# Reading the first 2048 rows of a row-sum as one contiguous block, and storing the sums in two pieces

## Chip, cores, metric

One core of one Trainium2 chip runs the kernel. The metric is the device time in microseconds (us) of one execution, lower is better. The granted clock was 1.0.

## The reference

```python
def setup_inputs():
    batch, seq, dim = 32, 512, 1024
    return {"x": np.random.randn(batch, seq, dim).astype(np.float32)}

def reference(x):
    return np.sum(np.maximum(x, 0), axis=-1).astype(np.float32)
```

There are 16384 rows of 1024 floats, 4 KB each: 64 MiB to read and 64 KB to write. Each row gives one sum of its positive elements.

## The kernel before

Each of the 128 partitions owns 128 consecutive rows. Its rows therefore begin 512 KB after those of the partition before it; I call this distance the *pitch*. A load of 16 rows for all partitions moves 8 MiB: from each partition's region it takes one contiguous run of 64 KB. Seven such loads go round three buffers; then come loads of 8, 4, 2 and 1 rows, and two halves of the last row.

```python
xv = x.rearrange("b s d -> (b s) d").rearrange("(p j) d -> p j d", p=P)
ov = out.rearrange("b s -> (b s)").rearrange("(p j) -> p j", p=P)
# ... buffers, semaphores (cut)
for c in range(NBIG + 1):                       # NBIG = 7, NB = 3, BIG = 16
    if c >= NB:
        sp.wait_ge(s_dve, 3 * (c - NB + 1))     # buffer free?
    if c < NBIG:
        sp.dma_start(
            out=buf[:, c % NB, :, :], in_=xv[:, c * BIG : (c + 1) * BIG, :]
        ).then_inc(s_in[c], 16)
# ... small loads of the tail, all issued at once; compute on ACT and DVE (cut)
sp.wait_ge(s_tdve, 1)
sp.dma_start(out=ov[:, :], in_=res[:, :]).then_inc(s_out, 16)
sp.wait_ge(s_out, 16)
```

Of the kernel before, what the change touches and what calls it, by code (L numbers as in the profile page):

```python
# [2 lines left out]

P = 128
D = 1024
BIG = 16
NBIG = 7
NTWO = 6
NB = 3
STEPS = [4, 5, 7]  # L10
MIXED = [3, 4, 5]
TAIL = [8, 4, 2, 1]
LAST = [512, 512]


def bass_relu_sum_kernel(
    nc: bass.Bass,
    x: bass.AP,
    out: bass.AP,
):  # L20





    fp32 = mybir.dt.float32
    ALU = mybir.AluOpType
    AF = mybir.ActivationFunctionType
    X = mybir.AxisListType.X

    B, S, _ = x.shape
    J = B * S // P
    assert BIG * NBIG + sum(TAIL) + 1 == J and sum(LAST) == D

    xv = x.rearrange("b s d -> (b s) d").rearrange("(p j) d -> p j d", p=P)
    ov = out.rearrange("b s -> (b s)").rearrange("(p j) -> p j", p=P)

    buf = nc.alloc_sbuf_tensor("buf", [P, NB, BIG, D], fp32)
    last = nc.alloc_sbuf_tensor("last", [P, LAST[1] + 1], fp32)
    res = nc.alloc_sbuf_tensor("res", [P, J], fp32)  # L40

    n_in = NBIG + len(TAIL) + 2
    s_in = [nc.alloc_semaphore(f"s_in{i}") for i in range(n_in)]
    s_act = nc.alloc_semaphore("s_act")
    s_dve = nc.alloc_semaphore("s_dve")
    s_tact = nc.alloc_semaphore("s_tact")
    s_tdve = nc.alloc_semaphore("s_tdve")
    s_out = nc.alloc_semaphore("s_out")

    sp, act, dve = nc.sync, nc.scalar, nc.vector  # L50


    tb = NBIG % NB
    for c in range(NBIG + 1):
        if c >= NB:
            sp.wait_ge(s_dve, 3 * (c - NB + 1))
        if c < NBIG:
            sp.dma_start(  # L58
                out=buf[:, c % NB, :, :], in_=xv[:, c * BIG : (c + 1) * BIG, :]
            ).then_inc(s_in[c], 16)  # L60
    r = 0
    tail = []
    for i, n in enumerate(TAIL):
        sp.dma_start(  # L64
            out=buf[:, tb, r : r + n, :],
            in_=xv[:, NBIG * BIG + r : NBIG * BIG + r + n, :],
        ).then_inc(s_in[NBIG + i], 16)
        tail.append((r, n, s_in[NBIG + i]))
        r += n
    sp.dma_start(  # L70
        out=buf[:, tb, r, 0 : LAST[0]], in_=xv[:, J - 1, 0 : LAST[0]]
    ).then_inc(s_in[-2], 16)
    sp.dma_start(out=last[:, 0 : LAST[1]], in_=xv[:, J - 1, LAST[0] : D]).then_inc(
        s_in[-1], 16
    )


    def on_act(t, acc):
        return act.activation(t, t, AF.Relu, accum_out=acc)  # L79

    def on_dve(t, acc):
        return dve.tensor_scalar(  # L82
            out=t, in0=t, scalar1=0.0, scalar2=None, op0=ALU.max, op1=ALU.add, accum_out=acc
        )

    def row(c, i):
        return buf[:, c % NB, i, :], res[:, c * BIG + i : c * BIG + i + 1]

    for c in range(NTWO):
        b, steps = c % NB, STEPS if c < NTWO - 1 else MIXED  # L90
        act.wait_ge(s_in[c], 16)
        if steps is MIXED:
            dve.wait_ge(s_in[c], 16)
            for i in (BIG - 4, BIG - 3):
                on_dve(*row(c, i))
        r = 0
        for i, n in enumerate(steps):
            t = buf[:, b, r : r + n, :]
            act.activation(t, t, AF.Relu).then_inc(s_act, 1)  # L99
            dve.wait_ge(s_act, 3 * c + i + 1)  # L100
            dve.tensor_reduce(  # L101
                out=res[:, c * BIG + r : c * BIG + r + n], in_=t, axis=X, op=ALU.add
            ).then_inc(s_dve, 1)
            r += n
        if steps is MIXED:
            for i in (BIG - 2, BIG - 1):
                on_act(*row(c, i))


    j0 = NBIG * BIG  # L110
    for c in range(NTWO, NBIG):
        act.wait_ge(s_in[c], 16)
        dve.wait_ge(s_in[c], 16)
        for i in range(BIG):
            (on_act if i % 2 else on_dve)(*row(c, i))
    for r, n, s in tail:
        if n > 1:
            act.wait_ge(s, 16)
        dve.wait_ge(s, 16)
        for i in range(r, r + n):  # L120
            f = on_act if (i - r) % 2 else on_dve
            f(buf[:, tb, i, :], res[:, j0 + i : j0 + i + 1])

    act.wait_ge(s_in[-2], 16)
    on_act(buf[:, tb, BIG - 1, 0 : LAST[0]], last[:, LAST[1] : LAST[1] + 1]).then_inc(s_tact, 1)
    dve.wait_ge(s_tact, 1)
    dve.wait_ge(s_in[-1], 16)
    on_dve(last[:, :], res[:, J - 1 : J]).then_inc(s_tdve, 1)


    sp.wait_ge(s_tdve, 1)
    sp.dma_start(out=ov[:, :], in_=res[:, :]).then_inc(s_out, 16)
    sp.wait_ge(s_out, 16)


# [1 line left out]
_INS = ['x']  # L137
_OUTS = [((32, 512), 'float32')]


# [21 lines left out]
```

## Time and profile before

| | before |
|---|---|
| median, first three runs | 162.84 us (162.80 to 163.05) |
| profiled span | 161.4 us |
| share of the chain that ended last | DMA 69%, ACT 18%, DVE 10% |
| one 64 KB packet once under way (the trace's DMA records) | 2.418 us |

The page of the kernel before: the DMA share by slices (in tenths, 40 slices), what was moved, and the parts of the chain that ended last.

```profile
DMA  7969979979979979979979979979979979899992
...
HBM read 67.11 MB, written 0.07 MB: 416 GB/s over the span
...
DMA 69%; ACT 18%; DVE 10%; SPq 1%; issue 0%
...
out_dram<-res SPq DMA_DIRECT2D x1, 64.0 KB, 1.5
```

The DMA engines are at it from the first slice to the last but one. The ACT and DVE shares of the chain are no proof of a compute limit: while these pieces ran, the next transfers were already queued. The last line says that the 64 KB store needs 1.5 us from issue to landing; it comes after everything else.

The table of stretches of the kernel before: start and end in us, length, then busy time of DVE, ACT and POOL, clock, DMA share and GB/s. This is the steady part.

```profile
23.10:42.40 19.30, 15.04 (x3) 14.04 (x3) 0.00 (x0) 1.00 1.00 435
42.40:61.90 19.50, 17.66 (x4) 14.07 (x4) 0.00 (x0) 1.00 1.00 430
61.90:81.20 19.30, 17.32 (x4) 14.02 (x3) 0.00 (x0) 1.00 1.00 435
```

DMA share 1.00 at 430 to 435 GB/s while ACT and DVE have time to spare: the loads bound the kernel. The Trainium skill ("DMA: Bandwidth & Descriptors", "Specifications") gives a fabric ceiling of 435 GB/s; sixteen engines at 64 KB in 2.418 us are 434 GB/s, so this trace agrees.

The timeline of the kernel before (start, length, engine, instruction, idle time before it and what ended it): ACT begins the first three transfers as soon as each has landed; the last line is its start on the seventh, which it takes row by row.

```profile
23.13 14.04 ACT L99 ACTIVATE buf<-buf 128x4096 f32<-128x4096 f32 x3 [21.13 <-DMA buf<-in_x_dram]
...
42.44 14.04 ACT L99 ACTIVATE buf<-buf 128x4096 f32<-128x4096 f32 x3 [5.26 <-DMA buf<-in_x_dram]
...
61.88 14.04 ACT L99 ACTIVATE buf<-buf 128x4096 f32<-128x4096 f32 x3 [5.40 <-DMA buf<-in_x_dram]
...
139.27 1.06 ACT L79 ACTIVATE buf<-buf 128x1024 f32<-128x1024 f32 x1 [6.64 <-DMA buf<-in_x_dram]
```

*First data* is ACT's first start, 23.13 us. *Later loads* is the time from there to the start on the seventh transfer at 139.27, 116.14 us: six steps, from the first transfer's landing to the seventh's.

The stretches around the start of the kernel before:

```profile
1.60:2.30 0.70, 0.00 (x0) 0.41 (x1) 0.00 (x0) 1.00 2.79 936
2.30:3.10 0.80, 0.00 (x0) 0.00 (x0) 0.00 (x0) 1.00 1.31 492
```

A packet is booked whole in the stretch where it begins; this is why the share exceeds 1. So the last column counts starts: 492 GB/s x 0.80 us is 6 packets of 64 KB. Six of the 16 DMA engines began their first packet only after 2.3 us; the other ten had begun between 1.73 and 2.3. I call these six *late starts*.

### The profile page before, as it was taken

The numbers are of one execution on the slowest core, as the hardware profiler recorded it, in microseconds if no ns is written. First come the engines' busy times: TensorE is split into PE (matmuls) and PEld (weight loads), VectorE is DVE, ScalarE is ACT, GpSimd is POOL, SyncE is SP. The second block draws the span as 40 slices with busy tenths as digits, with TensorE's granted clock in tenths as the row PEclk, the third lists the DMA queues.
The fourth block names the chain that finished last, engine by engine and source line by source line (L and its number), as shares of the span: only waits on it lengthen the run. The fifth ranks groups of instructions, "written<-read, shape, count | busy, mean of one in ns | idle before, by whom it ended". The sixth has DMA issues, their size and how long they took to land.

```text
span 161.4 us, 143 instructions
## 1 busy us (share of the span) xinstructions
DVE 122.0 (76%) x56; ACT 101.0 (63%) x55; POOL 0.2 (0%) x4
## 2 busy tenths in 40 slices
DVE  0000003998969898798979989699899999598995
ACT  3000029992499906998089960999429980496972
POOL 0000000000000000000000000000000000000000
DMA  7969979979979979979979979979979979899992
GB/s 260 504 292 504 471 341 487 487 325 487 487 325 487 471 309 520 471 309 520 487 309 504 487 325 487 487 325 487 487 325 487 487 325 487 374 422 414 406 406 74
DMA packets 2016, 67.18 MB, mean 416 GB/s; under 512 B 224, under 2 KB 352, under 8 KB 736
## 3 DMA queue, kind: packets, MB, share of 16 engines
q1 hardware_dynamic: 2016, 67.18, 97.0%
HBM read 67.11 MB, written 0.07 MB: 416 GB/s over the span
## 4 chain that ended last, share of the span: by engine, by line
DMA 69%; ACT 18%; DVE 10%; SPq 1%; issue 0%
DMA buf<-in_x_dram 69%; ACT buf L99 17%; DVE res L101 9%; SPq L64 1%; ACT buf L79 0%; DVE last L82 0%; SPq L58 0%
## 5 line engine op out<-in xcount | busy, mean ns | idle before, releaser
L101 DVE TENSOR_REDUCE res<-buf 128x4 f32<-128x4096 f32 (+3 forms) x18 | 100.4, 5603 | 34.9 <-ACT buf L99 34.9
L99 ACT ACTIVATE buf<-buf 128x4096 f32<-128x4096 f32 (+3 forms) x18 | 80.8, 4553 | 47.7 <-DMA buf<-in_x_dram 47.7
L79 ACT ACTIVATE buf<-buf 128x1024 f32<-128x1024 f32 (+1 forms) x18 | 18.4, 1021 | 9.7 <-DMA buf<-in_x_dram 9.7
L82 DVE TENSOR_SCALAR_CACHE_REDUCE buf<-buf 128x1024 f32<-128x1024 f32 x18 | 21.0, 1217 | 2.7 <-DMA buf<-in_x_dram 2.5
L79 ACT ACTIVATION_READ_ACCUMULATOR buf<-buf 128x1 f32 x18 | 3.4, 187 | 0.0
L99 ACT ACT_TABLE_LOAD x1 | 1.3, 1283 | 0.7 <-PEq L147 0.7
L82 DVE DVE_READ_ACCUMULATOR buf<-buf 128x1 f32 x18 | 1.5, 84 | 0.0
L82 DVE TENSOR_SCALAR_CACHE_REDUCE last<-last 128x513 f32<-128x513 f32 x1 | 0.7, 690 | 0.2 <-ACT buf L79 0.2
L147 POOL MEMSET const-bfloat16-1.0<- 128x1 bf16 x1 | 0.1, 102 | 0.0
L147 POOL MEMSET const-uint8-127<- 128x1 uint8 x1 | 0.1, 101 | 0.0
L147 POOL MEMSET const-float32-0.0<- 128x1 f32 x1 | 0.1, 99 | 0.2 <-issue 0.2
L147 POOL MEMSET const-float32-1.0<- 128x1 f32 x1 | 0.1, 98 | 0.0
L82 DVE DVE_READ_ACCUMULATOR last<-last 128x1 f32 x1 | 0.1, 83 | 0.0
## 6 DMA issues: line engine op xcount, KB each, us to landing
buf<-in_x_dram SPq DMA_DIRECT2D x1, 4096.0 KB, 26.7
buf<-in_x_dram SPq DMA_DIRECT2D x1, 2048.0 KB, 31.2
buf<-in_x_dram SPq DMA_DIRECT2D x1, 1024.0 KB, 33.2
buf<-in_x_dram SPq DMA_DIRECT2D x1, 512.0 KB, 34.0
buf<-in_x_dram SPq DMA_DIRECT2D x1, 256.0 KB, 34.1
last<-in_x_dram SPq DMA_DIRECT2D x1, 256.0 KB, 34.3
buf<-in_x_dram SPq DMA_DIRECT2D x7, 36.4
out_dram<-res SPq DMA_DIRECT2D x1, 64.0 KB, 1.5
```

Of the source, the lines that this page charges most:

```text
L64: sp.dma_start(out=buf[:, tb, r : r + n, :], in_=xv[:, NBIG * BIG + r : NBIG * BIG + r + n, :],).then_inc(s_in[NBIG + i], 16)
L79: return act.activation(t, t, AF.Relu, accum_out=acc)
L82: return dve.tensor_scalar(out=t, in0=t, scalar1=0.0, scalar2=None, op0=ALU.max, op1=ALU.add, accum_out=acc)
L99: act.activation(t, t, AF.Relu).then_inc(s_act, 1)
L101: dve.tensor_reduce(out=res[:, c * BIG + r : c * BIG + r + n], in_=t, axis=X, op=ALU.add).then_inc(s_dve, 1)
L147: nc = _bacc.Bacc("TRN2", target_bir_lowering=False, num_devices=1)
```

## The change

The first transfer reads rows 0 to 2047 as one block: 16 rows for each partition, pitch 64 KB. The other 14336 rows are dealt out 112 to a partition, pitch 448 KB. The sums then belong to two regions of the output, hence two stores: the first block's sums (64 B of each partition) are stored early, behind the queued loads, and the others (448 B of each partition instead of 512 B) at the end. The intent can only be at the ends of the load stream, since amount, packet size and compute stay.

```diff
-    xv = x.rearrange("b s d -> (b s) d").rearrange("(p j) d -> p j d", p=P)
-    ov = out.rearrange("b s -> (b s)").rearrange("(p j) -> p j", p=P)
+    xr = x.rearrange("b s d -> (b s) d")
+    of = out.rearrange("b s -> (b s)")
+    x0 = xr[0 : P * BIG, :].rearrange("(p j) d -> p j d", p=P)
+    o0 = of[0 : P * BIG].rearrange("(p j) -> p j", p=P)
+    xv = xr[P * BIG :, :].rearrange("(p j) d -> p j d", p=P)
+    ov = of[P * BIG :].rearrange("(p j) -> p j", p=P)
 ... (semaphore s_out0: cut)
-                out=buf[:, c % NB, :, :], in_=xv[:, c * BIG : (c + 1) * BIG, :]
+                out=buf[:, c % NB, :, :],
+                in_=xv[:, (c - 1) * BIG : c * BIG, :] if c else x0[:, :, :],
 ... (the tail's row numbers less BIG: cut)
+    sp.dma_start(out=o0[:, :], in_=res[:, 0:BIG]).then_inc(s_out0, 16)
 ...
-    sp.dma_start(out=ov[:, :], in_=res[:, :]).then_inc(s_out, 16)
+    sp.dma_start(out=ov[:, :], in_=res[:, BIG:J]).then_inc(s_out, 16)
+    sp.wait_ge(s_out0, 16)
     sp.wait_ge(s_out, 16)
```

More of the change, by code (lines that the diff above doesn't have):

```diff
@@ L47, in bass_relu_sum_kernel @@
     s_tdve = nc.alloc_semaphore("s_tdve")
+    s_out0 = nc.alloc_semaphore("s_out0")
     s_out = nc.alloc_semaphore("s_out")
@@ L65, in bass_relu_sum_kernel @@
             out=buf[:, tb, r : r + n, :],
-            in_=xv[:, NBIG * BIG + r : NBIG * BIG + r + n, :],
+            in_=xv[:, (NBIG - 1) * BIG + r : (NBIG - 1) * BIG + r + n, :],
         ).then_inc(s_in[NBIG + i], 16)
@@ L70, in bass_relu_sum_kernel @@
     sp.dma_start(
-        out=buf[:, tb, r, 0 : LAST[0]], in_=xv[:, J - 1, 0 : LAST[0]]
+        out=buf[:, tb, r, 0 : LAST[0]], in_=xv[:, J - BIG - 1, 0 : LAST[0]]
     ).then_inc(s_in[-2], 16)
-    sp.dma_start(out=last[:, 0 : LAST[1]], in_=xv[:, J - 1, LAST[0] : D]).then_inc(
+    sp.dma_start(out=last[:, 0 : LAST[1]], in_=xv[:, J - BIG - 1, LAST[0] : D]).then_inc(
         s_in[-1], 16
     )
+    sp.dma_start(out=o0[:, :], in_=res[:, 0:BIG]).then_inc(s_out0, 16)
     def on_act(t, acc):
```

## The prediction

> **What bounds the kernel now.** The loads do. In the chain that ended last, DMA has 69% of the span, and its ACT (18%) and DVE (10%) pieces run while later loads are already queued (waits view: ACT waited 47.7 us for loads). The table of stretches shows 430 to 435 GB/s and a DMA share of 1.00 from 23.1 to 120 us. Work on successive 8 MB transfers starts at 23.13, 42.44, 61.88, ..., 139.27 (timeline): 19.3 to 19.4 us each. In the trace's DMA records one 64 KB packet takes 2.418 us almost without exception after the first transfer; 16 engines at that pace are 433 GB/s. Only the two ends can give: the start (first load issued 0.73, usable 23.13, so 22.4 us against 19.35 for later ones: 3.05 us more) and the end (last load usable 158.31, span 161.4: 3.1 us).
>
> **The start in detail (DMA records).** The 16 engines' first packets begin between 1.73 and 2.97 us. The first packet on each took 2.49 to 3.27 us instead of 2.42, and six engines had a slow fifth packet (2.63 to 2.82). The excess over eight regular packets is 0.08 to 1.08 us by engine; the engine that finishes the first transfer last lost 0.76. With no excess and the same starts the transfer would end 34.12 − 33.64 = about 0.5 us earlier (estimate from those records). The engines are busy to the end, so a gain here is kept.
>
> **What the change does.** Bytes, packet size, load count and compute stay. The first transfer's row groups lie 64 KB apart instead of 512 KB; the later ones 448 KB apart. The Trainium skill, "DMA: Bandwidth & Descriptors", section "Latency and other measured facts", reports slow copies at power-of-two row pitches; its inference is channel aliasing of streams in lock step. This trace shows full rate at the 512 KB pitch except in the first packets, when the engines have just started together: estimate −0.1 to −0.5 us, or nothing if that is a cold start which any address pays. The steady part cannot gain.
>
> **The stores.** One more issue on SP (0.4 us) falls in its 34.7 us wait: free. The early store queues behind the last loads and should be done before 160.5. The last store stays on the path: issued 159.79, landed 1.5 us later, 128 runs of 512 B at 27 ns each. It becomes 128 runs of 448 B. The same page, "Specifications", says that below 512 B the DMA engine does a read-modify-write; nothing in this trace shows its cost. Estimate: +0 to +0.5 us (eight runs per engine, up to treble their 27 ns, plus a read).
>
> **Sum.** −0.1 to −0.5 and +0 to +0.5: 162.84 becomes about 162.6 us, 80% range 161.7 to 163.4. Chances: faster by over 2% 0.02, within 2% 0.96, slower by over 2% 0.02.
>
> **What would show each step.** Right: later transfers still 19.3 to 19.4 us apart; the first usable data at 22.6 to 23.0 instead of 23.13; last load to last store issue unchanged (1.5 us); final store 1.5 to 2.0 us to landing. Wrong: first data at 23.1 or later (cold start, not addresses); slow packets reappearing in the second transfer, which is then the first to touch the spread rows; a store above 2 us.
>
> **What would make it wrong.** The engines' late starts may themselves depend on the addresses (gain up to 1 us); neighbouring streams may collide and lengthen the first transfer by microseconds; the early store's short writes may still be in the way of the last one.

## The result, and the profile after

| | before | after | ratio, 95% interval |
|---|---|---|---|
| first comparison | 162.94 us (4 runs) | 162.38 us (4 runs) | 0.9964 [0.9947, 0.9982] |
| repeated later, run r2_after_again | 162.84 us (9 runs) | 162.38 us (5 runs) | 0.9973 [0.9960, 0.9987] |

A ratio is the mean time of one kernel's runs over that of the other's runs of the same rounds, so it is not quite the ratio of the medians quoted. The change is worth 0.44 to 0.59 us (0.27% and 0.36% of about 163 us): clear of the noise. The answering lines of the page after:

```profile
DMA  7979979979979979979979979979979969999992
...
HBM read 67.11 MB, written 0.07 MB: 417 GB/s over the span
...
DMA 69%; ACT 18%; DVE 10%; SPq 1%; issue 0%
...
out_dram<-res SPq DMA_DIRECT2D x1, 56.0 KB, 1.6
```

At this scale nothing has changed. The last store needs 1.6 us where the old one needed 1.5, but before rounding these are 1.56 and 1.54 (issue in the timeline to the last landing record), so the store is hardly longer. The timeline after, same rows as before:

```profile
22.77 14.04 ACT L107 ACTIVATE buf<-buf 128x4096 f32<-128x4096 f32 x3 [20.77 <-DMA buf<-in_x_dram]
...
42.12 14.05 ACT L107 ACTIVATE buf<-buf 128x4096 f32<-128x4096 f32 x3 [5.31 <-DMA buf<-in_x_dram]
...
61.47 14.04 ACT L107 ACTIVATE buf<-buf 128x4096 f32<-128x4096 f32 x3 [5.30 <-DMA buf<-in_x_dram]
...
138.89 1.06 ACT L87 ACTIVATE buf<-buf 128x1024 f32<-128x1024 f32 x1 [6.65 <-DMA buf<-in_x_dram]
```

First data comes at 22.77 instead of 23.13, 0.36 us earlier. The step from the second transfer to the third is 61.47 - 42.12 = 19.35 us instead of 61.88 - 42.44 = 19.44. The sum of later loads is 116.12 instead of 116.14. The stretches around the start, after:

```profile
1.60:2.30 0.70, 0.00 (x0) 0.41 (x1) 0.00 (x0) 1.00 4.40 1498
2.30:3.10 0.80, 0.00 (x0) 0.00 (x0) 0.00 (x0) 1.00 0.00 0
```

All 16 engines begin before 2.3 us; there is no late start. The spans, 161.4 and 161.0 us, differ by about what was won at the first data (0.36 us); the end costs the same: from the landing of the last load on the slowest engine to the end of the span the traces have 161.37 - 158.92 = 2.45 us before and 161.04 - 158.57 = 2.47 after.

But this is one trace of each. What has made the start earlier, and whether that is all, had to be tried.

### The profile page after: what moved, and what is told of

The parts are those of the page before. It is cut to its first block, busy times and chain, and to the rows that moved or that the text cites. A ratio compares the mean times of both kernels' runs of the same rounds, so it can differ in the third digit from the quotient of the medians.

```text
span 161.0 us, 144 instructions
## 1 busy us (share of the span) xinstructions
DVE 122.0 (76%) x56; ACT 101.0 (63%) x55; POOL 0.2 (0%) x4
## 4 chain that ended last, share of the span: by engine, by line
DMA 69%; ACT 18%; DVE 10%; SPq 1%; issue 0%
DMA buf<-in_x_dram 69%; ACT buf L107 17%; DVE res L109 9%; SPq L71 1%; ACT buf L87 0%; DVE last L90 0%; SPq L64 0%
```

## The experiments

Twelve kernels ran, in three calls; those of one call ran on one chip (e1 to e4; e7 to e10; r1, r2, e6 and e11). A ratio is always to the kernel before. For all but two runs (e9 and e10) I give it here and, from the trace, late starts (counted as above), first data and later loads:

| run | pitch of first / later transfers | ratio [95%] | late starts | first data, us | later loads, us |
|---|---|---|---|---|---|
| kernel before, first trace | 512 / 512 KB | 1 | 6 | 23.13 | 116.14 |
| r1_before_again | 512 / 512 | 1.0006 [0.9992, 1.0019] | 5 | 22.97 | 116.08 |
| e1_stores_only | 512 / 512 | 1.0011 [0.9998, 1.0024] | 6 | 22.96 | 116.58 |
| e8_later_448k | 512 / 448 | 0.9990 [0.9974, 1.0006] | 6 | 22.85 | 116.09 |
| changed kernel, first trace | 64 / 448 | 0.9964 [0.9947, 0.9982] | 0 | 22.77 | 116.12 |
| r2_after_again | 64 / 448 | 0.9973 [0.9960, 0.9987] | 2 | 22.68 | 116.08 |
| e2_block_only | 64 / 512 | 0.9971 [0.9958, 0.9985] | 2 | 22.66 | 116.43 |
| e3_block_second | 448, then 64 / 448 | 0.9969 [0.9956, 0.9981] | 0 | 22.73 | 116.12 |
| e7_pitch_508k | 508 / 512 | 0.9980 [0.9965, 0.9995] | 0 | 22.84 | 116.10 |
| e6_pitch_256k | 256 / 512 | 0.9991 [0.9978, 1.0004] | 2 | 22.82 | 116.08 |
| e4_one_block | 0 / 512 | 0.9971 [0.9954, 0.9988] | 0 | 22.01 | 116.42 |
| e11_first_row_alone | 64 / 448 | 0.9998 [0.9986, 1.0011] | not comparable | 22.90 | 116.10 |

My theory after the result was COMPACT: the first transfer now lies in 8 MB instead of being spread over 64 MB, and the engines get going together. The rivals were PITCH (512 KB between row groups is a bad distance, others are better), LATER (the gain is in the later transfers) and STORES.

**e1_stores_only**: loads as before, sums stored in two pieces.

```diff
+    sp.dma_start(out=ov[:, 0:BIG], in_=res[:, 0:BIG]).then_inc(s_out0, 16)
 ... (semaphore s_out0: cut)
-    sp.dma_start(out=ov[:, :], in_=res[:, :]).then_inc(s_out, 16)
+    sp.dma_start(out=ov[:, BIG:J], in_=res[:, BIG:J]).then_inc(s_out, 16)
+    sp.wait_ge(s_out0, 16)
```

> Loads as before, the two stores of the change (correct result). Theories of the 0.36% gain: COMPACT (the first transfer's small address range makes the engines start closer together), PITCH (512 KB between row groups collides, any other pitch is better), LATER (the gain is in the later transfers at 448 KB), STORES (the shorter last store). COMPACT, PITCH and LATER expect 162.8 to 163.1 here, ratio 1.000 within 0.001, first data at 23.1 us. STORES expects 162.4, ratio 0.9965.

Measured: 163.17 us, ratio 1.0011; six late starts and first data at 22.96. STORES falls: the gain is not there. Nor do the stores cost anything visible on the path: from the last load's landing to the end this trace has 161.65 - 159.21 = 2.44 us, against 2.45 before. The first-data expectation of 23.1 was missed by 0.14 us, which says how far single traces differ. Something unexpected: the second transfer took 19.71 us (the lines of the first three transfers in the timeline):

```profile
22.96 14.04 ACT L101 ACTIVATE buf<-buf 128x4096 f32<-128x4096 f32 x3 [20.95 <-DMA buf<-in_x_dram]
...
42.67 14.04 ACT L101 ACTIVATE buf<-buf 128x4096 f32<-128x4096 f32 x3 [5.67 <-DMA buf<-in_x_dram]
...
62.14 14.04 ACT L101 ACTIVATE buf<-buf 128x4096 f32<-128x4096 f32 x3 [5.43 <-DMA buf<-in_x_dram]
```

The DMA records show 18 packets over 2.5 us in this second transfer and 15 in the third. So the part that looked steady is not always steady. That loss is the trace of one execution.

**e2_block_only**: only the first transfer is the block; one store (wrong in 16 sums of each partition).

```diff
+    x0 = x.rearrange("b s d -> (b s) d")[0 : P * BIG, :].rearrange("(p j) d -> p j d", p=P)
-                out=buf[:, c % NB, :, :], in_=xv[:, c * BIG : (c + 1) * BIG, :]
+                out=buf[:, c % NB, :, :],
+                in_=xv[:, c * BIG : (c + 1) * BIG, :] if c else x0[:, :, :],
```

> Only the first transfer reads the contiguous 8 MB; the later ones stay at 512 KB pitch, one store (wrong on purpose in the first 16 sums of each partition). COMPACT and PITCH expect the whole gain: 162.4, ratio 0.9965, first data at 22.7 to 22.8 us, engines' first packets beginning within 0.6 us of each other instead of 1.2. LATER and STORES expect 162.9, ratio 1.000, first data at 23.1.

Measured: 162.50 us, ratio 0.9971, first data at 22.66, two late starts (the last at 2.75 us, so not within 0.6 us as expected):

```profile
2.30:3.10 0.80, 0.00 (x0) 0.00 (x0) 0.00 (x0) 1.00 0.41 164
...
22.66 14.04 ACT L101 ACTIVATE buf<-buf 128x4096 f32<-128x4096 f32 x3 [20.65 <-DMA buf<-in_x_dram]
```

The first transfer's addresses alone carry most of the gain, so LATER cannot be its whole source. In this trace the later loads took 116.43 us, 0.3 us longer than in the changed kernel: something is lost again at 512 KB, though the ratio, 0.9971, does not show it.

**e3_block_second**: the changed kernel with its first two loads exchanged, so that a transfer spread over 56 MB at 448 KB comes first (correct result).

```diff
-                in_=xv[:, (c - 1) * BIG : c * BIG, :] if c else x0[:, :, :],
+                in_=x0[:, :, :] if c == 1 else xv[:, max(c - 1, 0) * BIG : max(c, 1) * BIG, :],
+        k = (1 - c if c < 2 else c) * BIG
-                out=res[:, c * BIG + r : c * BIG + r + n], in_=t, axis=X, op=ALU.add
+                out=res[:, k + r : k + r + n], in_=t, axis=X, op=ALU.add
```

> The changed kernel with its first two loads in the other order: the first one is spread over 56 MB at 448 KB pitch, the contiguous block comes second (correct result). COMPACT expects the gain gone: 162.9, ratio 1.000, first data at 23.1. PITCH expects it kept: 162.4, ratio 0.9965, first data at 22.75. LATER expects it kept too.

Measured: 162.44 us, ratio 0.9969, no late start, first data at 22.73:

```profile
1.60:2.30 0.70, 0.00 (x0) 0.40 (x1) 0.00 (x0) 1.00 4.42 1498
2.30:3.10 0.80, 0.00 (x0) 0.00 (x0) 0.00 (x0) 1.00 0.00 0
...
22.73 14.04 ACT L108 ACTIVATE buf<-buf 128x4096 f32<-128x4096 f32 x3 [20.72 <-DMA buf<-in_x_dram]
```

COMPACT, my own theory, falls: contiguity is not needed. At a pitch of 448 KB a first transfer spread over 56 MB keeps the gain. Whether any pitch other than 512 KB would do is what e7 and e6 ask.

**e4_one_block**: the first transfer reads the same 64 KB for each partition (wrong).

```diff
+    x0 = x.rearrange("b s d -> (b s) d")[0:BIG, :].partition_broadcast(P)
 ... (load line as in e2_block_only)
```

> The first transfer reads the same 64 KB for each of the 128 partitions, the most compact source there is; the rest as before (wrong on purpose in the first 16 sums). COMPACT expects at least the gain of the change, 162.0 to 162.4, ratio 0.994 to 0.9965, and first packets near 2.42 us if their slowness has to do with touching new memory; if the slow first packet (2.8 to 3.3 us) is a start-up cost whatever the address, it stays at that. PITCH in its form 'streams in step meet in the same part of the memory' expects it slower than before: first data at 23.5 us or later, ratio above 1.002.

Measured: 162.31 us, ratio 0.9971. In the DMA records the first packets took 2.52 to 2.59 us, against 2.49 to 3.27 before and 2.82 to 3.63 after. First data came at 22.01, 0.65 us ahead of any kernel that reads distinct rows:

```profile
22.01 14.04 ACT L101 ACTIVATE buf<-buf 128x4096 f32<-128x4096 f32 x3 [20.00 <-DMA buf<-in_x_dram]
...
41.53 14.04 ACT L101 ACTIVATE buf<-buf 128x4096 f32<-128x4096 f32 x3 [5.48 <-DMA buf<-in_x_dram]
```

So the slow first packet is not a fixed cost of starting an engine: it depends on what the sixteen engines read. The expected loss from "streams in step meet in the same part of the memory" did not come; reading literally the same rows is fast. Part of the gain is given back: the second transfer took 19.52 us, against 19.31 to 19.35 in the four traces of the kernels before and after, and later loads 116.42.

**e7_pitch_508k** and **e6_pitch_256k**: the kernel before with the first transfer at another pitch (wrong); the load line is that of e2_block_only.

```diff
+    x0 = x.rearrange("b s d -> (b s) d")[0 : P * 127, :].rearrange("(p j) d -> p j d", p=P)[:, 0:BIG, :]   # e7
+    x0 = x.rearrange("b s d -> (b s) d")[0 : P * 64, :].rearrange("(p j) d -> p j d", p=P)[:, 0:BIG, :]    # e6
```

> The kernel before, with only the first transfer read at a pitch of 508 KB (127 rows) instead of 512 KB, as widely spread as before (wrong on purpose in the first 16 sums). After the run with the block in second place, COMPACT has fallen. PITCH expects the engines' first packets to begin within 0.5 us of each other (1.2 us before), first data at 22.6 to 22.8, and about 162.4 to 162.5 us, ratio 0.996 to 0.9975. A rival, that only the pitches 448 KB and 64 KB happen to suit, would leave starts and first data as before: 23.1, ratio 1.000.

> The kernel before with only the first transfer at 256 KB pitch (wrong on purpose). If it is the power of two that makes the engines meet, late starts stay (last one at 2.5 to 3.0), first data at 22.9 to 23.1, ratio 0.999 to 1.000. If only the full 512 KB is bad, it is as with 508 KB: starts to 2.1, ratio 0.997 to 0.998.

At 508 KB: 162.64 us, ratio 0.9980, clear of noise but just short of the 0.996 to 0.9975 that PITCH expected; no late start, as it expected:

```profile
1.60:2.30 0.70, 0.00 (x0) 0.41 (x1) 0.00 (x0) 1.00 4.58 1498
2.30:3.10 0.80, 0.00 (x0) 0.00 (x0) 0.00 (x0) 1.00 0.00 0
...
22.84 14.04 ACT L101 ACTIVATE buf<-buf 128x4096 f32<-128x4096 f32 x3 [20.83 <-DMA buf<-in_x_dram]
```

But first data came at 22.84, just short of the expected 22.6 to 22.8, and no earlier than with 512 KB on the same chip (22.85 in e8_later_448k). The DMA records show why: the first packets took 2.89 to 3.74 us, on average 3.20 (in e8_later_448k 3.00). Most of what was won at the start was paid in the first packet. The trace of the kernel before shows the other side of this: the ten engines that began early took 3.13 us on average for their first packet, the six late ones 2.80. So late starts alone do not explain the gain. At 256 KB the ratio of 0.9991 (its interval holds 1) and the last start at 2.66 us lie where the power-of-two expectation had them, and first data at 22.82 is 0.08 us earlier than it said; but there are two late starts and not five or six. It is not shown that powers of two are to blame: 64 KB is one too, and e2_block_only keeps the gain with it.

**e8_later_448k**: the changed kernel with the first transfer back at 512 KB (wrong).

```diff
-    x0 = xr[0 : P * BIG, :].rearrange("(p j) d -> p j d", p=P)
+    x0 = xr.rearrange("(p j) d -> p j d", p=P)[:, 0:BIG, :]
```

> The changed kernel with the first transfer put back to 512 KB pitch; the later transfers stay at 448 KB, two stores (wrong on purpose). PITCH of the first transfer expects first data back at 23.0 to 23.1 and most of the gain gone: 162.7 to 163.0, ratio 0.9985 to 1.000. LATER (packets over 2.5 us in transfers 2 to 4 at 512 KB, which neither kernel with 448 KB shows) expects 19.35 us from the second transfer on without exception, and 0.1 to 0.3 us of gain kept: ratio 0.998 to 0.9995. If the whole gain stays, 0.9965, the first transfer's pitch was not the cause.

Measured: 162.73 us, ratio 0.9990 [0.9974, 1.0006]. The six late starts are back:

```profile
1.60:2.30 0.70, 0.00 (x0) 0.40 (x1) 0.00 (x0) 1.00 2.70 936
2.30:3.10 0.80, 0.00 (x0) 0.00 (x0) 0.00 (x0) 1.00 1.38 492
...
22.85 14.04 ACT L107 ACTIVATE buf<-buf 128x4096 f32<-128x4096 f32 x3 [20.85 <-DMA buf<-in_x_dram]
```

Most of the gain is gone with them, going by the ratio itself; its interval is wide. First data at 22.85 is earlier than the expected 23.0 to 23.1. What is kept, some 0.16 us by the ratio, is not clear of noise, and 0.9990 lies in the range of LATER as well as in that of PITCH. From the second transfer on, each took 19.32 to 19.36 us.

**e9_touch_same** and **e10_touch_other**: the kernel before with a small load ahead, waited for, that reads 512 B for each partition: of the row groups that the first transfer will read, or of the first 128 rows of the input (one look each; about 2 us dearer on purpose).

```diff
+    sp.dma_start(out=last[:, 0:128], in_=xv[:, 0, 0:128]).then_inc(s_touch, 16)                               # e9
+    sp.dma_start(out=last[:, 0:128], in_=x.rearrange("b s d -> (b s) d")[0:P, 0:128]).then_inc(s_touch, 16)   # e10
+    sp.wait_ge(s_touch, 16)
 ... (semaphore s_touch: cut)
```

> The kernel before with a small load of the first 512 B of each of the 128 row groups, waited for, ahead of the first transfer (about 2 us dearer on purpose). One look at the packets. If the slow first packet (2.5 to 3.3 us) comes from the first touch of each address region, the first packets of the big transfer are now regular (2.42 to 2.5) and the late starts are gone. If it comes from 16 engines starting together on addresses that collide, it stays at 2.8 to 3.3 and starts still spread over 1.2 us.

> The same, but the small load reads the first 128 rows, one 512 KB stretch, so 127 of the 128 row groups stay untouched. First touch of addresses: first packets slow (2.8 to 3.3) here and regular in the run that touched the same groups. A cost of the queue's or engines' own first use: regular in both. Collision at a common start: slow in both.

Measured: 165.32 and 164.81 us. In the DMA records the first packets of the big transfer took 2.87 to 3.39 us in the one and 2.51 to 3.21 in the other; their starts were spread over 0.95 and 1.20 us. Both stay slow. So neither a first use of the engines nor a first touch of the row groups, as far as 512 B of each touches them, is the cause in these traces (one of each). Of the three expectations that leaves sixteen engines starting together on a set of addresses, which no run isolates. The small load itself gave a second sight of the pitch. Issue to landing, first with a pitch of 512 KB (e9_touch_same):

```profile
last<-in_x_dram SPq DMA_DIRECT2D x1, 64.0 KB, 2.5
```

and with 4 KB (e10_touch_other):

```profile
last<-in_x_dram SPq DMA_DIRECT2D x1, 64.0 KB, 2.0
```

The same 64 KB landed 0.5 us later with the 128 reads of 512 B lying 512 KB apart (one trace of each).

**r1_before_again** and **r2_after_again**: both kernels unchanged, for second traces and for the noise.

> The kernel before, unchanged, for a second trace and for the noise of the comparison: 162.9 to 163.1, ratio 1.000 within 0.001. TWO PARTS (the first transfer at 512 KB costs some 0.25 us by late starts, and the second to fourth transfers at 512 KB some 0.2 us by packets over 2.5 us) expects again engines' first packets up to 2.7 us or later, and from the first transfer's data to the last row of the seventh more than 116.12 us. CHANCE (one trace of each is too few) would show starts within 0.6 us here too.

> The changed kernel, unchanged: 162.4, ratio 0.9955 to 0.9975. TWO PARTS expects starts within 0.6 us, first data at 22.6 to 22.8, no packet over 2.5 us in transfers 2 to 6. CHANCE expects a ratio whose interval holds 1.

Ratios 1.0006 and 0.9973, so the difference is no accident of the first comparison. First data at 22.97 and 22.68 repeats 23.13 and 22.77 (first line r1_before_again, second r2_after_again):

```profile
22.97 14.04 ACT L99 ACTIVATE buf<-buf 128x4096 f32<-128x4096 f32 x3 [20.96 <-DMA buf<-in_x_dram]
...
22.68 14.04 ACT L107 ACTIVATE buf<-buf 128x4096 f32<-128x4096 f32 x3 [20.67 <-DMA buf<-in_x_dram]
```

CHANCE falls. Three details were missed: the kernel before had later loads of 116.08, not over 116.12, so its loss there does not occur in every execution; the changed kernel had two late starts, the last at 2.56 us, so its starts are not always within 0.6 us; and it had one packet of 2.52 us in the fifth transfer.

**e11_first_row_alone**: the changed kernel with the first transfer cut into 1 and 15 rows, a try at a better version (correct result).

```diff
+        if c == 0:
+            sp.dma_start(out=buf[:, 0, 0:1, :], in_=x0[:, 0:1, :]).then_inc(s_in[0], 16)
+            sp.dma_start(out=buf[:, 0, 1:BIG, :], in_=x0[:, 1:BIG, :]).then_inc(s_in[0], 16)
-        act.wait_ge(s_in[c], 16)
+        act.wait_ge(s_in[c], 16 if c else 32)
 ... (the other transfers' branch, now an elif: cut)
```

> The changed kernel with its first transfer cut into one row (4 KB) and fifteen rows (60 KB) for each partition, correct result: a try at a version better than both. If the slow first packets (2.8 to 3.6 us) come from 16 engines asking for 64 KB each at once, short packets first should let them slip out of step sooner: first data up to 0.4 us earlier, 162.0, ratio 0.994. If it is a ramp that any start pays, nothing changes: 162.4, ratio 0.9965, or slightly worse by the extra packets' overhead.

Measured: 162.80 us, ratio 0.9998. The gain of the change is lost. The first 4 KB packets took 0.16 to 0.78 us where the median of this size in the tail of the changed kernel is 0.16, and first data came at 22.90. Over its first transfer an engine lost 0.50 us on average in the 4 KB packets and another 0.41 us in the 60 KB ones, against their usual 0.16 and 2.27 us; in the changed kernel it lost 0.67 us. Short packets first do not get round the slow start. No version better than the changed kernel was found; e3_block_second equals it.

## Why the prediction was right or wrong

*What bounds the kernel* was right: the loads, at about 434 GB/s, before and after.

*The size* was right as a total: 162.6 predicted with 161.7 to 163.4, 162.38 measured, "within 2%". But the range of 1.7 us holds "no change" (162.84) too, so being inside it says nothing of the mechanism. The 162.6 is not the plain sum either: the middles of the two terms, -0.3 and +0.25, would give 162.8. The forecast gain of about 0.24 us was about half of the 0.44 to 0.59 us measured; three terms of the sum have to be looked at.

*The start, -0.1 to -0.5 us.* The size holds: over the traces with 64 KB first (22.77, 22.68, 22.66; mean 22.70) against those with 512 KB first (23.13, 22.97, 22.96, 22.85; mean 22.98) it is 0.28 us, and the two groups do not overlap; e1 against e2 on one chip gives 0.30, r1 against r2 on another 0.29. The way was wrong, so that the size came right was luck. The prediction said that the slow first packets, an excess over 2.42 us, were what could gain. They did not: the sixteen first packets average 3.03 us in the four traces with 512 KB first and 3.09 in the three with 64 KB. What moved was the *late starts*, five or six engines against none to two, and with them the spread between the first and the last engine to finish the first transfer (DMA records: 0.79 to 1.01 us against 0.55 to 0.76). Averaged over the sixteen engines, the first packet began at 2.14 us in the four traces and at 1.97 in the three, while the excess over eight regular packets was 0.67 and 0.68 us. The prediction had the late starts only as something that might make it wrong. Its note that the late starts "may themselves depend on the addresses" is what the runs showed. Its list of what would show each step did not catch the wrong way: first data at 22.77, the store at 1.6 us and the 1.5 us between last load and last store all came out as "right", because nothing in the list asked for the engines' starts.

*"The steady part cannot gain"* was too firm. At 512 KB some executions have packets over 2.5 us in the second to fourth transfer: six of the nine traces with 512 KB later show nine or more of them, the five with 448 KB not one. Later loads average 116.28 us in those nine (the seven of the table, and 116.33 and 116.32 of the two touch runs) and 116.10 in the five. That is some 0.18 us. As a time difference this term alone is not clear (0.9990, with an interval that holds 1). Whether it has to do with how close together the engines finish the first transfer stays open: of the three traces with the largest loss, two (e2_block_only and e4_one_block) are those with the closest finish, 0.56 and 0.43 us from first to last engine, but the third (e1_stores_only) had 0.81; at 448 KB a finish within 0.55 us (r2_after_again) cost nothing.

*The last store, +0 to +0.5 us*: no cost shows, in the traces or in e1_stores_only (1.0011; the interval would still allow 0.4 us). The Trainium skill ("DMA: Bandwidth & Descriptors", "Specifications") warns of read-modify-write below 512 B. In this trace the 448 B runs took 25 ns each (median), against 27 ns for 512 B, and the store 1.56 us instead of 1.54. The early store had landed by 158.75, before the last one was issued at 159.44.

Added up: 0.28 at the start and 0.18 later make 0.46 us, against 0.44 to 0.59 measured. This agreement is not proof that the account is closed. In the two pairs of traces of the unaltered kernels (23.13 and 22.77, 22.97 and 22.68) the start gave 0.36 and 0.29 us and the later loads 0.02 and 0.00. Of the single changes, the first transfer alone won 0.47 us (0.9971), the later pitch alone 0.16 (0.9990); together that is 0.63, more than was measured. And with the block first, the later pitch made no difference that shows (0.9971 at 512 KB, 0.9964 and 0.9973 at 448). What is shown is the first transfer's part; the later part is not shown as a time.

*Open.* Why a pitch of 512 KB makes engines start late, and why the first packets are slow whenever the engines read distinct rows, is not settled. The Trainium skill ("DMA: Bandwidth & Descriptors", "Latency and other measured facts") infers that streams in lock step alias in the memory channels at large power-of-two pitches. That 512 KB is worse than 448 KB fits it; 256 KB and 64 KB, powers of two as well, lay between or were good, and 508 KB cured the late starts without bringing first data forward. No run here looks into the memory, and none separates reading the rows from handing out the packets: a late start is time before an engine's first record begins, a slow packet time inside it.

## What to carry to other kernels

A kernel like this one, which streams at the DMA engines' pace and must move the same bytes, can be won or lost only at the ends and in irregular packets: count late starts and slow packets in the DMA records before believing that the steady part has nothing. When rows are dealt to 128 partitions, try more than one distance between them; here 448 KB or 64 KB instead of 512 KB for the first transfer bought 0.3%, while 256 KB bought nothing clear, and the contiguous block was only one way to get there. And test the obvious reading of a change by keeping the rest and exchanging the order: it took one run to show that contiguity was not needed.

## What the Trainium skill lacked or had wrong

- "DMA: Bandwidth & Descriptors", "Latency and other measured facts": its pitch entry is about copies between tensors, with 207 GB/s at 512 KiB against 214 as full rate. For loads it lacks that 512 KB still runs at about 434 GB/s once under way, that there is a loss in the start (0.28 us here, up to six of sixteen engines late), and that some executions have slow packets later (on average some 0.18 us over six transfers in the traces; not shown as a time). A 64 KB load in runs of 512 B landed after 2.5 us at 512 KB pitch and after 2.0 us at 4 KB.
- The same page, "Specifications": the 512 B limit. A store of 128 runs of 448 B had packets of 25 ns, against 27 ns for 512 B, and took 1.56 us instead of 1.54; no cost of read-modify-write shows at this size.
- No page that I read has the slow first packet at a common start: 2.5 to 3.7 us instead of 2.42 for 64 KB when the engines read distinct rows, 2.52 to 2.59 when all read the same rows, and not cured by a small load ahead.
